# A streaming encoder layer on one core: loads moved on SyncE's queue, operand splits spread, rows scaled by VectorE

## The chip, the cores and the metric

One core of a Trainium2 chip. Its engines run side by side, each through its own instruction queue in order: TensorE (PE; weight loads PEld), VectorE (DVE), ScalarE (ACT), GpSimd (POOL) and SyncE (SP), which here issues the DMA transfers. The metric is the device time of one execution in microseconds.

## The reference, cut to what matters

One layer over 2048 tokens of width 1024, all in float32:

```python
h = x * (1.0 + sc1) + sh1
proj = einsum('bsd,de->bse', h, w_in)             # u, q, k, v
y_pool = pool_mixer(u, w_pool, pool_scale)        # trailing means, 4 windows
y_attn = chunked_attention(q, k, v, rel_bias)     # 64-token chunks, 9-chunk band, 8 heads
y = einsum('bse,ed->bsd', concatenate([y_pool, y_attn]), w_out)
x = layer_norm(ALPHA * x + (1.0 + g1) * y, ln1_g, ln1_b)
h = x * (1.0 + sc2) + sh2
f = square(relu(einsum('bsd,df->bsf', h, w_ff1)))  # width 4096
f = einsum('bsf,fd->bsd', f, w_ff2)
x = layer_norm(ALPHA * x + (1.0 + g2) * f, ln2_g, ln2_b)
```

The six vectors sh, sc, g come from the conditioning vector c.

## The kernel before

A float32 product is made of three matmuls in a reduced type: each operand is split into a high part (ScalarE casts it) and a low part (VectorE, or GpSimd in the first stage, subtracts the high part from the source). `split` writes both; one split of a 128x1024 tile is one cast and one subtraction (L59, L60).

Four stages follow each other. The order of instructions on each engine is the order in which the code issues them; a helper `after(n, f)` keeps a call back until `tick` has counted n further steps.

1. **Input projection and attention** (to about 680 us). The change leaves it as it is.
2. **Output projection and first layer norm** (about 680 to 857 us): 16 tiles t of 128 tokens. Of each, two halves n of 512 columns are 24 matmuls each (`wout_half`, L385), then `residual` adds x (tile `xt`, L872), `ln1_head` takes statistics (VectorE), four values (GpSimd, L782 to L784) and the normalised rows n (ScalarE, L785). `ln1_turn(u)` transposes a tile u, three tiles behind t at first, on TensorE and scales it into `h` on ScalarE (L831). `ln1_sums(u)` makes, for tiles 4 to 7 of a half of the tokens, four combinations with the rows of the partner tile (`hp`, loaded by `ln1_load` into a tile named w, L821; combinations L854 to L857) for the seven-product scheme of the next stage. The projection's left operands are streamed: `Stream` loads item j+2 into one of two `raw` buffers as soon as item j has been split (`dma_to` in `split_some`, L74); item t+2 is split at the start of tile t.
3. **First half of the MLP** (about 857 to 1502 us): 32 groups g of hidden columns, and for each group seven products s (a seven-product scheme over 2x2 blocks; `product`, L1041, 12 matmuls each). Product s multiplies a weight piece (split by `w_split`) with operand s (`hslot[s]`), a split tile. Products 0, 2, 4, 6 add into one PSUM bank and 1 (alone), 3, 5 into others, so between them `evacuate` copies a bank out (ScalarE, L1048) or adds it to a copy (VectorE, L1054). Groups 0 to 15 use the first 1024 tokens, groups 16 to 31 the other tokens, whose seven operands lie in DRAM and are loaded and split by `refill(i)` while group 15 runs: the load at product (15, i), the two splits one product later. Operand 4 of the first tokens is loaded after tile 15 (`op_load(4)`) and split in product (0,1), operand 6 in (0,4).
4. **Second half of the MLP and second layer norm** (about 1502 us to the end): 56 groups e of 48 matmuls (`issue`, L1322), 28 for each half of the tokens. In group e four splits are issued for group e+2 (`f2_split`), loads go four items ahead. Eight rows tiles `acc` (four named acc, four in g) hold ALPHA * x scaled by ln1_g (`ag`) plus ALPHA * ln1_b (`ab`): `load_acc` loads a tile from xS and GpSimd multiplies and adds (L1279, L1280). `take` adds finished banks to them (L1327). From e = 24 on `finish` makes the second layer norm of a tile (statistics L1287, L1299, L1303), stores it and loads the other tokens' rows into its place. A list `todo` of such generators is worked off in up to four steps per group.

Of the kernel before, what the change touches and what calls it, by code (L numbers as in the profile page):

```python
# [8 lines left out]
F32 = mybir.dt.float32  # L9
# [15 lines left out]
def trunk_layer(ctx: ExitStack, tc: tile.TileContext, xT, x, wada1, wada2, vecs, rows, win, wfirst, wpT, wout,  # L25
# [36 lines left out]
    class Stream:  # L62
        def __init__(self):
            self.items, self.raw, self.hl = [], {}, {}
            self.n_dma = self.n_split = 0

        def add(self, src, low, mul=None, dst=None):
# [14 lines left out]
        def split_some(self, i):  # L82
            while self.n_split <= min(i, len(self.items) - 1):
                j = self.n_split
                self.n_split += 1
                self.dma_to(j)
                r = self.raw.pop(j)
                _, low, mul, dst = self.items[j]
                if mul is not None:
                    mul(r)  # L90
                hl = dst() if dst else stream.tile([128, 2, 1024], F32R, name="hl", tag="hl", bufs=3)
                self.hl[j] = hl
                for c in range(0, 1024, 512):
                    split(hl[:, 0, c:c + 512], hl[:, 1, c:c + 512], r[:, c:c + 512], low)
                    yield
                self.dma_to(j + 2)

# [17 lines left out]
    late = {}  # L115
# [238 lines left out]
    def run(g):  # L354
        for _ in g:
            pass
# [418 lines left out]

    def norm(z, n):
        s6 = small.tile([128, 2, 6], F32, name="s6", bufs=3)
        for i in range(2):
            nc.vector.bn_stats(s6[:, i, :], z[:, i * 512:i * 512 + 512])
        mv = small.tile([128, 4], F32, name="mv", bufs=3)  # L780
        nc.vector.bn_aggr(mv[:, 0:2], s6)
        nc.gpsimd.tensor_scalar(mv[:, 1:2], mv[:, 1:2], EPS, 1.0, op0=ALU.add, op1=ALU.mult)  # L782
        nc.gpsimd.tensor_tensor(mv[:, 2:3], mv[:, 1:2], mhalf, op=ALU.pow)
        nc.gpsimd.tensor_scalar(mv[:, 3:4], mv[:, 0:1], mv[:, 2:3], -1.0, op0=ALU.mult, op1=ALU.mult)  # L784
        nc.scalar.activation(n, z, AF.Identity, bias=mv[:, 3:4], scale=mv[:, 2:3])  # L785

# [87 lines left out]
    def ln1_head(t):  # L874
        n_tiles[t] = ln.tile([128, 1024], F32, name="n", bufs=3)
        norm(xt.pop(t), n_tiles[t])
        if t + 2 < 16:
# [48 lines left out]

    def op_load(i):

        ops[i] = []
        for c in range(2):  # L930
            r = stream.tile([128, 1024], F32, name="raw", tag="raw", bufs=2).rearrange("p (r k c) -> p r k c", r=2, k=4)
            nc.sync.dma_start(r, h_piece(0, i, 2 * c, 2))
            ops[i].append(r)
# [17 lines left out]
    TURNS = {t: (t - 3,) if t < 11 else (2 * t - 14, 2 * t - 13) if t < 13 else (t - 1,) for t in range(3, 15)}  # L951
    waiting = []
    for t in range(3, 15):
        yc = st.get(yi[t]).rearrange("p a (k c) -> p a k c", k=8)
# [27 lines left out]
    ps = [dbank() for _ in range(2)]  # L982
    ln1_load(14)
    w_split(0, 0)
    for kh in range(2):
# [3 lines left out]
        if kh == 0:  # L989
# [3 lines left out]
            op_split(3)  # L993
            w_split(0, 1)
        tick(6)
    for n in range(2):
# [3 lines left out]
    w_load(1, late["w"])  # L1000
    op_load(4)
    ln1_sums(14, 1)
# [132 lines left out]

    def refill(i):

        hslot[i] = slot(i, "h2")
        if i % 2:
            r = ffp.tile([128, 4, 4, 128], F32, name="tw", tag="tw", bufs=1)  # L1140
            nc.sync.dma_start(r, h_piece(1, i, 0, 4))
            parts = [r[:, 0:2], r[:, 2:4]]
        else:
            parts = []
            for c in range(2):
                r = stream.tile([128, 1024], F32, name="raw", tag="raw", bufs=2).rearrange("p (r k c) -> p r k c", r=2, k=4)
                nc.sync.dma_start(r, h_piece(1, i, 2 * c, 2))
                parts.append(r)
        yield
        for c in range(2):  # L1150
            op_put(i, c, parts[c])

    back, refills = [], []

# [28 lines left out]
    for g in range(32):  # L1183
        for s in range(7):
            product(g, s)
            tick()
            if g == 0:
                if s == 1:
                    op_split(4)
                    ln1_load(15)  # L1190
                    op_load(6)
                elif s == 2:
# [32 lines left out]
            evacuate(g, s)  # L1225
            if (g, s) == (0, 0):
                w_split(0, 2)

# [16 lines left out]
            if back and next(back[0], "end") == "end":  # L1245
                back.pop(0)
            if (g == 15 and s) or (g, s) == (16, 0):
                if refills:
                    run(refills.pop())
            if g == 15:  # L1250
                refills.append(refill(s))
                next(refills[0])
            if g == 31 and s >= 3:
# [21 lines left out]
    def load_acc(b, t):  # L1275
        acc[t] = f2l.tile([128, 1024], F32, name=f"acc{t}") if t < 4 else gs[:, 2 * t - 8:2 * t - 6, :].rearrange(
            "p a c -> p (a c)")
        nc.sync.dma_start(acc[t], xS[b][t * 128:t * 128 + 128, :])
        nc.gpsimd.tensor_mul(acc[t], acc[t], late["ag"])  # L1279
        nc.gpsimd.tensor_add(acc[t], acc[t], late["ab"])  # L1280

# [47 lines left out]
    def finish(b, t):  # L1329
# [5 lines left out]
        outs.pop(t)()  # L1335
        yield

    todo = []
    for b in range(2):
        for i in range(7):  # L1340
            for kq in range(4):
# [18 lines left out]
                if e == 1:  # L1360
# [3 lines left out]
                    for t in range(8):  # L1364
                        load_acc(0, t)
                if e == 2:
                    late["l2g"] = row(f2l, rows[4:5], "r1")
                    late["l2b"] = row(f2l, rows[5:6], "r2")
                for _ in range(4):
                    if todo and next(todo[0], "end") == "end":  # L1370
                        todo.pop(0)
# [62 lines left out]
```

## Time and profile before

| | |
|---|---|
| median of three runs | 2141.13 us (2140.64 to 2142.0) |
| the profiled execution | 2148.31 us, span 2146.5 us |
| mean granted TensorE clock | 0.988 |
| TensorE busy | 2054.8 us (96%) |
| VectorE busy | 1324.2 us (62%) |
| ScalarE busy | 1002.8 us (47%) |
| GpSimd busy | 429.5 us (20%) |

The times of single instructions come from the profiled execution, and its span with what lies around it is 7.2 us over the median. TensorE's matmuls are pipelined, so a busy TensorE isn't by that at its best pace; the number of matmuls in stretches of equal length tells more. A wait is put down to what ended last before it. Idle time of the other engines costs nothing by itself.

### The profile page before, as it was taken

The numbers are of one execution on the slowest core, as the hardware profiler recorded it, in microseconds if no ns is written. First come the engines' busy times: TensorE is split into PE (matmuls) and PEld (weight loads), VectorE is DVE, ScalarE is ACT, GpSimd is POOL, SyncE is SP. The second block draws the span as 40 slices with busy tenths as digits, with TensorE's granted clock in tenths as the row PEclk, the third lists the DMA queues.
The fourth block names the chain that finished last, engine by engine and source line by source line (L and its number), as shares of the span: only waits on it lengthen the run. The fifth ranks groups of instructions, "written<-read, shape, count | busy, mean of one in ns | idle before, by whom it ended". The sixth has DMA issues, their size and how long they took to land. (4 is left out here: it accounts for less than half of the span.)

```text
span 2146.5 us, 27078 instructions
## 1 busy us (share of the span) xinstructions
PE 2054.8 (96%) x9672; PEld 1691.9 (79%) x9672; DVE 1324.2 (62%) x1926; ACT 1002.8 (47%) x1592; POOL 429.5 (20%) x474
## 2 busy tenths in 40 slices
PE   7999989999999999899999899999999999989998
PEld 6778867888877877678887788888778888878886
DVE  7555555556664454777767666666595449974448
ACT  4454555555553536545555555555444333343330
POOL 1535353553332000000000000000360004510002
PEclk9999999999999999999999999999999999999999
DMA  7444443444433557878878888887967556675542
GB/s 295 137 134 124 149 139 108 134 124 131 127 124 111 182 191 305 302 266 311 295 278 300 275 287 282 302 291 262 354 216 245 190 177 216 225 274 184 189 167 108
DMA packets 210361, 456.69 MB, mean 213 GB/s; under 512 B 18609, under 2 KB 36529, under 8 KB 209202
## 3 DMA queue, kind: packets, MB, share of 16 engines
q1 hardware_dynamic: 210226, 454.96, 62.5%
q8 instruction: 76, 1.25, 0.2%
q14 instruction: 59, 0.48, 0.1%
HBM read 294.45 MB, written 152.05 MB: 208 GB/s over the span
## 5 line engine op out<-in xcount | busy, mean ns | idle before, releaser
L1322 PE MATMUL f<-sb,sa 128*128 128x512 f32 x2688 | 624.7, 395 | 10.4 <-DVE sb L60 10.0
L1322 PEld LDWEIGHTS f<-sb,sa 128*128 128x128 f32 x2688 | 507.6, 189 | 127.3 <-DVE sb L60 12.4
L421 PE MATMUL d<-hT,hl 128*128 128x512 f32 x1392 | 373.0, 400 | 1.9 <-ACT vt L316 1.9
L1041 PE MATMUL f<-h,hl 128*128 128x512 f32 x1536 | 364.6, 393 | 6.2 <-ACT c L1048 6.2
L1041 PEld LDWEIGHTS f<-h,hl 128*128 128x128 f32 x1536 | 289.8, 189 | 72.3 <-ACT c L1048 7.0
L1041 PE MATMUL f<-sb,hl 128*128 128x512 f32 x1152 | 281.6, 398 | 10.3 <-ACT c L1048 6.2
L421 PEld LDWEIGHTS d<-hT,hl 128*128 128x128 f32 x1392 | 248.9, 189 | 42.3 <-ACT vt L316 2.3
L1041 PEld LDWEIGHTS f<-sb,hl 128*128 128x128 f32 x1152 | 219.4, 191 | 61.5 <-ACT c L1048 7.5
L635 DVE TENSOR_TENSOR PT<-T,PT 128x640 fp32r<-128x640 f32 (+4 forms) x128 | 94.9, 741 | 217.9 <-ACT PT L634 215.8
L612 ACT ACTIVATE s<-s,m 128x640 f32<-128x640 f32 (+4 forms) x128 | 98.0, 765 | 221.9 <-DVE m L610 170.8
L385 PE MATMUL d<-hT,hl 128*128 128x512 f32 x696 | 169.0, 400 | 4.1 <-DVE xt L872 4.1
L1063 ACT ACTIVATE g<-g 128x512 f32<-128x512 f32 x96 | 60.8, 633 | 211.6 <-DVE g L1054 211.6
L385 PEld LDWEIGHTS d<-hT,hl 128*128 128x128 f32 x696 | 131.5, 192 | 32.1 <-DVE xt L872 4.3
L618 POOL TENSOR_SCALAR s<-s,m 128x640 f32<-128x640 f32 (+4 forms) x128 | 96.5, 754 | 241.7 <-DVE m L617 199.2
L59 ACT CAST sb<-hl 128x1024 fp32r<-128x1024 f32 x67 | 70.4, 1050 | 152.2 <-PE f L1322 128.8
L60 DVE TENSOR_TENSOR sb<-hl,sb 128x1024 fp32r<-128x1024 f32 x67 | 95.1, 1420 | 73.8 <-ACT sb L59 73.5
L60 DVE TENSOR_TENSOR hl<-wsum,hl 128x1024 fp32r<-128x1024 f32 x64 | 78.4, 1225 | 95.2 <-ACT hl L59 95.1
L1363 POOL TENSOR_SCALAR ag<-ag 128x1024 f32<-128x1024 f32 x1 | 1.3, 1306 | 673.2 <-DMA acc<-xS 673.2
L60 DVE TENSOR_TENSOR sb<-raw,sb 128x1024 fp32r<-128x1024 f32 x55 | 84.6, 1544 | 54.7 <-ACT sb L59 54.5
L59 ACT CAST sb<-raw 128x1024 fp32r<-128x1024 f32 x55 | 57.4, 1051 | 114.1 <-PE f L1322 87.7
L1291 POOL TENSOR_SCALAR zv<-zv 128x1 f32<-128x1 f32 x16 | 18.4, 1150 | 449.8 <-DVE zv L1290 449.8
L60 DVE TENSOR_TENSOR hl<-w,hl 128x1024 fp32r<-128x1024 f32 x64 | 61.3, 958 | 70.0 <-ACT hl L59 70.0
(178 smaller groups left out, 2785.4 us busy)
## 6 DMA issues: line engine op xcount, KB each, us to landing
fS<-g SPq DMA_DIRECT2D x224, 256.0 KB, 3.6
hl<-fS SPq DMA_DIRECT2D x67, 512.0 KB, 4.6
hl<-tS SPq DMA_DIRECT2D x67, 512.0 KB, 4.5
w<-in_w_dram SPq DMA_DIRECT2D x48, 512.0 KB, 4.2
raw<-fS SPq DMA_DIRECT2D x45, 512.0 KB, 4.5
raw<-tS SPq DMA_DIRECT2D x45, 512.0 KB, 4.5
wS<-wsum SPq DMA_DIRECT2D x32, 512.0 KB, 4.9
raw<-in_w_dram SPq DMA_DIRECT2D x32, 512.0 KB, 5.3
```

Source lines behind the costliest of these rows:

```text
L59: nc.scalar.copy(hl_h, src)
L60: low.tensor_sub(hl_l, src, hl_h.bitcast(F32))
L385: nc.tensor.matmul(ps, yc[:, a, k, :], hT(b, k, cols), start=(k == 0 and i == 0), stop=(k == 7 and i == 2))
L421: nc.tensor.matmul(ps, w[name][:, a, k, :], hT(b, k, slice(tb * 512, tb * 512 + 512)), start=(n == 0), stop=(n == 23))
L612: nc.scalar.activation(s[:, 0:w], s[:, 0:w], AF.Exp, bias=m[:, 0:1], scale=-1.0, accum_out=m[:, 1:2])
L618: nc.gpsimd.tensor_scalar(s[:, 0:nk * 128], s[:, 0:nk * 128], m[:, 1:2], 1.0, op0=ALU.mult, op1=ALU.mult)
L635: nc.vector.tensor_sub(ol, src, oh.bitcast(F32))
L1041: nc.tensor.matmul(ps, w[:, p, c:c + 128], h[:, q, k, :], start=first and k == 0 and (p, q) == (0, 0), stop=k == 3 and p == 1, skip_group_ ...
L1063: nc.scalar.activation(o, o, AF.Relu)
L1291: nc.gpsimd.tensor_scalar(mv[:, 1:2], mv[:, 1:2], EPS, 1.0, op0=ALU.add, op1=ALU.mult)
L1322: nc.tensor.matmul(bank, f, w, start=start, stop=stop, skip_group_check=True)
L1363: nc.gpsimd.tensor_scalar(r, r, ALPHA, 1.0, op0=ALU.mult, op1=ALU.mult)
```

## The change

Four things.

- **Stream loads.** In stage 2 `Stream.defer` becomes `after(6, f)`: the load of item j+2 is issued at the end of the first half of tile t rather than directly behind the split at its start.
- **Operand 4 and tile 15.** Operand 4 of the first tokens is loaded into one tile of the ring `n` at the start of tile 15 and one of the ring `xt` in its middle, and split directly behind `ln1_head(15)`. `op_load(6)` takes the old place of `op_load(4)`. `norm` now returns the normalising activation instead of issuing it, and for tile 15 it is issued behind the copy of product (0,0).
- **Other tokens' operands.** `refill` is gone. With q = 7 (g - 15) + s counting products from (15,0), loads stand at q = -2, -1, 2, 4, 6, 7, 9 and the splits at q = 1, 3, 5, 6, 8, 10, 11. Operand i is used at q = 7 + i.
- **Rows.** The multiplication and the addition on `acc` move from GpSimd to VectorE, as two steps of a generator `scale_acc` in `todo`. Three steps are worked off per group from e = 4 to 51, four otherwise, and a generator that ends no longer uses up a step.

```diff
+            self.defer = lambda f: f()
@@ split_some
-                self.dma_to(j + 2)
+                self.defer(lambda: self.dma_to(j + 2))
@@ norm
-        nc.scalar.activation(n, z, AF.Identity, bias=mv[:, 3:4], scale=mv[:, 2:3])
+        return lambda n: nc.scalar.activation(n, z, AF.Identity, bias=mv[:, 3:4], scale=mv[:, 2:3])
@@ ln1_head
-        norm(xt.pop(t), n_tiles[t])
+        apply = norm(xt.pop(t))
+        if t == 15:
+            late["n"] = lambda: apply(n_tiles[t])
+        else:
+            apply(n_tiles[t])
@@ op_load
-        for c in range(2):
-            r = stream.tile([128, 1024], F32, name="raw", tag="raw", bufs=2).rearrange("p (r k c) -> p r k c", r=2, k=4)
-            nc.sync.dma_start(r, h_piece(0, i, 2 * c, 2))
+        for t in tiles or [stream.tile([128, 1024], F32, name="raw", tag="raw", bufs=2) for _ in range(2)]:
+            r = t.rearrange("p (r k c) -> p r k c", r=2, k=4)
+            nc.sync.dma_start(r, h_piece(0, i, 2 * len(ops.setdefault(i, [])), 2))
...
+    st.defer = lambda f: after(6, f)
     for t in range(3, 15):
...
     ln1_load(14)
+    op_load(4, [ln.tile([128, 1024], F32, name="n", bufs=3)])
     w_split(0, 0)
...
             op_split(3)
             w_split(0, 1)
+            op_load(4, [ln.tile([128, 1024], F32, name="xt", bufs=2)])
...
     w_load(1, late["w"])
-    op_load(4)
+    op_load(6)
+    op_split(4)
     ln1_sums(14, 1)
@@ refill becomes refill_load (the loads alone)
+    LOADS = {-2: 0, -1: 1, 2: 2, 4: 3, 6: 4, 7: 5, 9: 6}
+    SPLITS = {1: 0, 3: 1, 5: 2, 6: 3, 8: 4, 10: 5, 11: 6}
@@ loop over g and s
                 if s == 1:
-                    op_split(4)
                     ln1_load(15)
-                    op_load(6)
...
             if (g, s) == (0, 0):
+                late["n"]()
                 w_split(0, 2)
...
-            if (g == 15 and s) or (g, s) == (16, 0):
-                if refills:
-                    run(refills.pop())
-            if g == 15:
-                refills.append(refill(s))
-                next(refills[0])
+            q = 7 * (g - 15) + s
+            if q in SPLITS:
+                op_split(SPLITS[q])
+            if q in LOADS:
+                refill_load(LOADS[q])
@@ load_acc
-        nc.gpsimd.tensor_mul(acc[t], acc[t], late["ag"])
-        nc.gpsimd.tensor_add(acc[t], acc[t], late["ab"])
+
+    def scale_acc(t):
+        nc.vector.tensor_mul(acc[t], acc[t], late["ag"])
+        yield
+        nc.vector.tensor_add(acc[t], acc[t], late["ab"])
+        yield
@@ finish
         outs.pop(t)()
         yield
+        if b == 0:
+            yield from scale_acc(t)
@@ loop over e
                     for t in range(8):
                         load_acc(0, t)
+                        todo.append(scale_acc(t))
...
-                for _ in range(4):
-                    if todo and next(todo[0], "end") == "end":
+                for _ in range(4 if e < 4 or e >= 52 else 3):
+                    while todo and next(todo[0], "end") == "end":
                         todo.pop(0)
```

What moves, in the order of the queues. SyncE, stage 2, around tile 9; raw<-yS is the stream load, w<-hP the partner's rows, xS and hP are stores. Before:

```order
L761 DMA xt_7174<-in_x_dram 128x1024
L74 DMA raw_7228<-yS1_66 128x1024
L821 DMA w_7230<-hP00_81 128x1024
L825 DMA xS0_125<-n_7014 128x1024
L862 DMA hP02_83<-w_7126 128x1024
L863 DMA hP01_82<-w_7164 128x1024
L761 DMA xt_7279<-in_x_dram 128x1024
```

Now:

```order
L762 DMA xt_7172<-in_x_dram 128x1024
L75 DMA raw_7174<-yS1_66 128x1024
L822 DMA w_7228<-hP00_81 128x1024
L826 DMA xS0_125<-n_7014 128x1024
L863 DMA hP02_83<-w_7124 128x1024
L864 DMA hP01_82<-w_7162 128x1024
L762 DMA xt_7277<-in_x_dram 128x1024
L75 DMA raw_7279<-yS1_66 128x1024
```

The raw load that a tile's own split releases stood ahead of that tile's w load (raw_7228 ahead of w_7230); now it stands five rows later, behind the next xt load (raw_7279 behind w_7228), and the raw load ahead of the w load is the one of the tile before.

ScalarE at the passage from stage 2 to stage 3: `sb<-raw` and `sb<-n`, `sb<-xt` are casts of operands, `n<-xt` the normalisation of tile 15, `c<-f` the copy of product (0,0), `h<-T` the scaling behind the transposes of tile 15. Before:

```order
L59 CAST sb<-raw 128x2x4x128 x2
L59 CAST hl<-wsum 128x1024
L785 ACTIVATE n<-xt,mv 128x1024
L1048 COPY c<-f 128x512
L59 CAST hl<-wsum 128x1024
L59 CAST sb<-raw 128x2x4x128 x2
L831 ACTIVATE h<-T,b_6606,a_6605 128x128 x8
```

Now:

```order
L59 CAST sb<-raw 128x2x4x128 x2
L59 CAST hl<-wsum 128x1024
L59 CAST sb<-n 128x2x4x128
L59 CAST sb<-xt 128x2x4x128
L1056 COPY c<-f 128x512
L786 ACTIVATE n<-xt,mv 128x1024
L59 CAST hl<-wsum 128x1024
L832 ACTIVATE h<-T,b_6606,a_6605 128x128 x8
```

Operand 4's casts moved from behind the copy to ahead of it, the normalisation from ahead to behind.

VectorE in stage 4, where the first half's tiles are finished (sa, sb are splits, ag and ab the scaling of a reloaded row, n<-g and n<-n the layer norm). Before:

```order
L1287 BN_STATS z_14687<-acc_13060 128x6 x2
L1290 BN_AGGR zv<-z_14687 128x2
L1299 SCALAR_TENSOR_TENSOR n<-acc_13060,zv,r_13149 128x1024
L1303 SCALAR_TENSOR_TENSOR n<-n,zv,r_13151 128x1024
L60 TENSOR_TENSOR sa<-hl,sa 128x1024
L60 TENSOR_TENSOR sb<-hl,sb 128x1024
L60 TENSOR_TENSOR sa<-hl,sa 128x1024
L60 TENSOR_TENSOR sb<-raw,sb 128x1024
```

Now:

```order
L1296 BN_STATS z_14981<-acc_13062 128x6 x2
L1299 BN_AGGR zv<-z_14981 128x2
L1308 SCALAR_TENSOR_TENSOR n<-acc_13062,zv,r_13137 128x1024
L1312 SCALAR_TENSOR_TENSOR n<-n,zv,r_13139 128x1024
L60 TENSOR_TENSOR sa<-hl,sa 128x1024
L60 TENSOR_TENSOR sb<-hl,sb 128x1024
L60 TENSOR_TENSOR sa<-raw,sa 128x1024
L60 TENSOR_TENSOR sb<-raw,sb 128x1024
L1286 TENSOR_TENSOR acc_14991<-acc_14991,ag 128x1024
L1288 TENSOR_TENSOR acc_14991<-acc_14991,ab 128x1024
L1296 BN_STATS z_15061<-g 128x6 x2
L1299 BN_AGGR zv<-z_15061 128x2
```

Between the splits of two groups stood one tile's layer norm; now three steps stand there, of which the scaling of a reloaded row makes two.

## Rows read from the trace of the kernel before

**Rows 1.** Waits of TensorE: total us, times, longest us.

```profile
PE f L1041 <- ACT c L1048: 12.4, 5, 3.6
PE f L1322 <- DVE sb L60: 10.0, 6, 6.0
```

**Rows 2.** Stretches: length, busy us (count) by engine, clock, DMA share, GB/s.

```profile
1050.00:1100.00 50.00, 50.00 (x220) 40.98 (x219) 37.62 (x51) 23.98 (x37) 0.00 (x0) 1.00 0.77 273
...
1150.00:1200.00 50.00, 44.38 (x181) 35.55 (x180) 35.40 (x40) 33.52 (x44) 0.00 (x0) 0.93 0.88 310
1200.00:1250.00 50.00, 47.84 (x202) 38.67 (x202) 31.94 (x41) 25.02 (x38) 0.00 (x0) 0.97 0.82 285
...
1550.00:1600.00 50.00, 47.78 (x206) 38.27 (x205) 46.63 (x23) 20.21 (x20) 39.34 (x13) 1.00 0.65 221
...
1600.00:1650.00 50.00, 50.00 (x220) 41.04 (x219) 33.55 (x33) 24.63 (x24) 0.00 (x0) 1.00 0.73 252
...
1850.00:1900.00 50.00, 44.04 (x181) 35.59 (x180) 45.37 (x34) 16.18 (x16) 23.27 (x12) 0.93 0.70 237
...
1950.00:2000.00 50.00, 50.00 (x216) 40.51 (x215) 21.55 (x20) 18.13 (x18) 0.00 (x0) 1.00 0.54 179
```

**Rows 3.** Timeline of TensorE, stages 2 to 3: start, length us; idle before, releaser.

```profile
794.27 7.38 PE L385 MATMUL d<-hT,hl 128*128 128x512 f32 x24 [4.11 <-DVE xt L872]
...
811.59 1.45 PE L828 MATMUL T<-ident,n 128*128 128x128 f32 x8 [3.54 <-ACT w L831]
...
866.70 4.62 PE L1041 MATMUL f<-h,hl 128*128 128x512 f32 x12 [3.61 <-ACT c L1048]
...
877.41 4.41 PE L1041 MATMUL f<-sb,hl 128*128 128x512 f32 x12 [2.46 <-ACT c L1048]
```

**Rows 4.** Timeline of TensorE, group 15, products 5 and 6.

```profile
1175.90 2.93 PE L1041 MATMUL f<-h,hl 128*128 128x512 f32 x12
1181.87 5.49 PE L1041 MATMUL f<-sb,hl 128*128 128x512 f32 x12 [3.04 <-DVE g L1054]
```

**Rows 5.** Timeline of SyncE's queue in stage 2.

```profile
776.16 0.32 SPq L74 DMA_DIRECT2D raw<-yS  x1
776.58 0.38 SPq L821 DMA_DIRECT2D w<-hP  x1
...
793.65 0.32 SPq L74 DMA_DIRECT2D raw<-yS  x1
...
850.97 0.32 SPq L825 DMA_DIRECT2D xS<-n  x1
```

**Rows 6.** Timeline of VectorE in stage 2: the first combination behind the w load.

```profile
783.75 0.69 DVE L854 TENSOR_TENSOR w<-w 128x512 f32<-128x512 f32 x1 [6.42 <-issue]
```

**Rows 7.** Tile acc: time from a load's issue to its landing.

```profile
DMA to landing us min/median/max: 3.3/6.3/11.1
```

**Rows 8.** Timeline of ScalarE between stages 2 and 3.

```profile
864.94 1.24 ACT L785 ACTIVATE n<-xt,mv 128x1024 f32<-128x1024 f32 x1 [7.03 <-POOL mv L784]
866.08 0.56 ACT L1048 COPY c<-f 128x512 f32<-128x512 f32 x1
```

**Rows 9.** Timeline of ScalarE in group 15: the casts of operand 3.

```profile
1182.96 1.99 ACT L59 CAST sb<-tw 128x1024 fp32r<-128x1024 f32 x2 [3.20 <-DMA tw<-hP]
```

**Rows 10.** Timeline of VectorE in stage 4, groups 25 to 27.

```profile
1784.50 3.43 DVE L60 TENSOR_TENSOR sa<-raw,sa 128x1024 fp32r<-128x1024 f32 x1
...
1791.22 1.27 DVE L1287 BATCH_NORM_STATS2 z<-acc 128x6 f32<-128x512 f32 x2
...
1797.12 1.22 DVE L60 TENSOR_TENSOR sb<-hl,sb 128x1024 fp32r<-128x1024 f32 x1
...
1804.96 1.27 DVE L1287 BATCH_NORM_STATS2 z<-acc 128x6 f32<-128x512 f32 x2
```

**Rows 11.** Timeline of GpSimd in stage 4: the first scaling, and one of a reloaded row.

```profile
1540.66 2.41 POOL L1279 TENSOR_TENSOR acc<-acc,ag 128x1024 f32<-128x1024 f32 x1
...
1784.07 2.78 POOL L1279 TENSOR_TENSOR acc<-acc,ag 128x1024 f32<-128x1024 f32 x1 [3.08 <-DMA acc<-xS]
```

More of the change, by code (lines that the diff above doesn't have):

```diff
@@ L774, in trunk_layer, with norm @@
     nc.vector.tensor_add(b2, b2, mods[:, 0, :])
-    def norm(z, n):
+    def norm(z):
         s6 = small.tile([128, 2, 6], F32, name="s6", bufs=3)
@@ L925, in trunk_layer, with op_load @@
     ops = {}
-    def op_load(i):
-        ops[i] = []
-        for c in range(2):
-            r = stream.tile([128, 1024], F32, name="raw", tag="raw", bufs=2).rearrange("p (r k c) -> p r k c", r=2, k=4)
-            nc.sync.dma_start(r, h_piece(0, i, 2 * c, 2))
+    def op_load(i, tiles=()):
+        for t in tiles or [stream.tile([128, 1024], F32, name="raw", tag="raw", bufs=2) for _ in range(2)]:
+            r = t.rearrange("p (r k c) -> p r k c", r=2, k=4)
+            nc.sync.dma_start(r, h_piece(0, i, 2 * len(ops.setdefault(i, [])), 2))
             ops[i].append(r)
@@ L1134, in right_halves, with refill_load @@
             nc.sync.dma_start(tS[i][p], s)
-    def refill(i):
-        hslot[i] = slot(i, "h2")
+    LOADS = {-2: 0, -1: 1, 2: 2, 4: 3, 6: 4, 7: 5, 9: 6}
+    SPLITS = {1: 0, 3: 1, 5: 2, 6: 3, 8: 4, 10: 5, 11: 6}
+    def refill_load(i):
         if i % 2:
@@ L1141, in refill @@
             nc.sync.dma_start(r, h_piece(1, i, 0, 4))
-            parts = [r[:, 0:2], r[:, 2:4]]
+            ops[i] = [r[:, 0:2], r[:, 2:4]]
         else:
-            parts = []
+            ops[i] = []
             for c in range(2):
@@ L1147, in refill @@
                 nc.sync.dma_start(r, h_piece(1, i, 2 * c, 2))
[L1148 to L1153, printed above, removed]
+                ops[i].append(r)
+    back = []
     f2_items = [(b, i, kq, c, kind) for b in range(2) for i in range(7) for kq in range(4) for c in range(2)
```

## The prediction

> **What bounds the kernel now.** TensorE: it is busy 96% of the span and issues at a fixed pace, so I looked for the stretches in which it doesn't. First the list of what it waited for [rows 1]: the long entries are ScalarE's copies out of PSUM between the seven products, and VectorE's splits in the last stage. Then the stretches of equal length [rows 2]: undisturbed ones hold 220 matmuls in 50 us, so one costs 50 / 220 = 0.2273 us. The two from 1150 to 1250 us hold 57 too few, 1550 to 1600 holds 14 too few, 1850 to 1900 holds 39 too few. Such a stretch has two losses: the wait, and TensorE's clock, whose mean is 0.93 in two of them against 1.00. Twelve matmuls take 2.93 us at the full clock, and 4.62 us right after a wait of 3.61 us [rows 3, 4]: behind a wait of over 2 us I add 1.7 us. From 1950 us on a third thing shows: 216 matmuls in 50 us, at a clock of 1.00 and with no wait [rows 2]. This slow pace follows the stretch at 1850.
>
> **Part 1, stream loads half a tile later.** In the projection stage SyncE's queue holds, tile by tile, the load into raw and then the load of the partner rows into w. The raw load can't issue before a split has emptied its buffer, and the w load stands behind it: it issued at 776.58 us, right after raw at 776.16; the next raw load issued at 793.65, 17.49 us later [rows 5]. VectorE waited 6.42 us for those rows, until 783.75 us [rows 6]; only behind its four combinations stand the tile's statistics, GpSimd's three small steps, ScalarE's normalisation and the next split. So the circle split, raw load, w load, combination, split takes 17.5 us, while a tile's 48 matmuls and 8 transposes take 48 x 0.2273 plus about 1, some 12 us. TensorE's waits of 4.11 and 3.54 us [rows 3] are this lag. In the new order raw stands behind xt, so the w load stands behind a split of the tile before. The raw load is still one and a half tiles (18 us) ahead of its use, and landings of 512 KB took 3.3 to 11.1 us [rows 7]. Without the 6.42 us the circle is 17.49 - 6.42 = 11.1 us, under 12. Gain: 4.11 + 3.54 + 2 x 1.7 = **11.05 us**. Late next is the same circle, with 1 us to spare; if the w load is held by the store that frees its tile instead, the gain goes to 0.
>
> **Part 2, operand 4 early, normalisation of tile 15 late.** Product (0,2) adds into the bank that ScalarE must first copy out. ScalarE stood at the normalisation of tile 15 (n<-xt), which started at 864.94 us after 7.03 us of waiting for GpSimd; the copy started at 866.08 [rows 8], and product (0,2) at 866.70 after 3.61 us [rows 3]. Product (0,0) had ended one product earlier than that wait began, at 863.1 - 2.9 = 860.2. Now two casts of operand 4 stand ahead of the copy and the normalisation behind it. They need a load into n and one into xt; the second is queued on SyncE behind the store of tile 14, which issued at 850.97 [rows 5]. If it lands within some 7 us the copy is on time; if it takes 11.1, copy, normalisation and the cast of wsum stand behind it and most of the old wait is back. What is late next: the transposes of tile 15 need the normalisation at about 866.2, 0.5 us after product (0,2) ends. The 2.46 us in front of product (0,4) [rows 3] stay, since its copy stands behind those transposes in both orders. On VectorE the two splits move ahead of ln1_sums(14) and of the split of wsum, 2.4 us that pass before product (0,4) needs them. The loads of operand 6 move up and meet a free raw buffer. Gain: 3.61 + 1.7 - 0.5 = **4.8 us** (0 to 6).
>
> **Part 3, operands of the second half over eleven products.** Before, all seven are loaded and split while products (15,0) to (16,0) run. A split is two casts (1.99 us) and two subtractions (1.22 us each); ScalarE stood 3.20 us waiting for one load [rows 9, 10]. The copies and additions that free the banks stood behind, and TensorE waited, 3.04 us among others [rows 4]. The loss is 57 x 0.2273 = 13.0 us. The work stays: 14 casts, 14 us, on top of ScalarE's usual 23.98 in 50 us [rows 2], 14.4 in the 30 us of eleven products. Going through the new order product by product with these durations I get four waits: 0.4 us in front of (15,6), whose bank waits for an addition behind operand 1; 1.5 in front of (16,2), whose copy stands behind the casts of operand 3; 1.2 at (16,5), since operand 5 is cast only when (16,3) has been copied out and takes 0.2 + 0.5 + 2.0 + 1.2 = 3.9 us against one product of 2.7; and 1.9 at (16,6) for operand 6, which follows it through both engines. Sum 5.0 us, each too short for the clock as I take it. Gain **8.0 us**. Ends: 13.0 if these overlap better than worked out, 3.1 if a load is late by 3.20 us again and one wait brings the clock down (5.0 + 3.2 + 1.7 left).
>
> **Part 4, rows scaled by VectorE.** GpSimd made 32 operations on 128x1024 rows. While one runs, a split's subtraction takes 3.43 us, alone 1.22 [rows 10]. One finished tile took VectorE 1804.96 - 1791.22 = 13.74 us [rows 10], more than a group's 48 x 0.2273 = 10.9, so its lead shrank until TensorE stood for 6.0 us [rows 1]. Now: 13.74 - 2 x (3.43 - 1.22) + 2 x 1.22 = 11.8 us per finished tile, 4.9 of it four splits; a tile takes five steps at three per group, so a group costs 4.9 + 0.6 x 6.9 = 9.0 us of 10.9. The added wait: each multiplication stands on VectorE until its row is loaded, and the splits, hence TensorE, stand behind it. For five of the second half's eight tiles the order puts load and multiplication into the same group. GpSimd waited 3.08 us for such a row [rows 11], landings were 3.3 to 11.1 [rows 7]: 15 to 55 us in all, against 1.9 us per group over 13 groups (25 us) and a lead of two groups (22 us). Mostly covered. In the first half VectorE waits in group 1 until the first row is there, 1540.66 us at the latest [rows 11], again with a lead of two groups. So both losses go: 14 x 0.2273 = **3.2 us** and 39 x 0.2273 = **8.9 us**. The slow pace (50 / 216 - 50 / 220 = 4.2 ns a matmul, for the 1030 from there to the end) began with the wait, and I take it to go too: **4.3 us**, or 0.
>
> **Sum.** 11.05 + 4.8 + 8.0 + 3.2 + 8.9 + 4.3 = 40.2 us. The profiled execution took 2148.31 us, 7.2 above the median of 2141.13; it would come to 2108.1, the median to **2100.9 us**.
>
> **Rivals.** (a) The pace stays at 216 whatever the waits: 2105.2. For it: no row shows its cause. Against: it begins with the wait. (b) Part 3 makes new waits with late loads: 2100.9 + 4.9 = 2105.8. For it: ScalarE is at 14 + 14.4 of 30 us there. (c) The w load of part 1 waits for its own tile's store: 2112. Against: that store is issued a tile earlier. (d) Reloads at the head of VectorE's queue use up its lead, and much of the 8.9 and the 4.3 us stays: about 2110. (e) VectorE becomes the bound of the last stage: if the 32 operations, 32 x 1.22 = 39 us, all lengthen the path in place of the 12.1 us of waits, the time is 2141.1 - 23.9 + 26.9 = 2144. Against: the subtraction of 3.43 us beside GpSimd. A rule for it, in the Trainium skill, "Perfetto Trace Analysis", section Optimizing Scalar/DVE Operations: a saturated VectorE may be relieved by moving work to GpSimd, the reverse of this part, though, it adds, the two share a read port and it might not help. By that first half the time would be this rival's; the row of 3.43 us sides with the second.
>
> (f) Slower: the mechanism of (d) at full size. If each of the eight reloads holds VectorE for its landing w, 8w less the 47 us of cover falls on TensorE; from w = 10.4 us on that eats parts 1 to 3, the 3.2 and the 8.9 us (36 us), from 10.9 on the kernel is 0.2% slower, and at 11.1 it takes 2147 us. Only the longest landing is that long [rows 7]. That the change doesn't do what it says I leave out: the order shows each move.
>
> **Chances.** Forecast 0.50; (a) 0.17, (b) 0.11, (c) 0.08, (d) 0.07, (e) 0.02, two or more of (a) to (d) together (2110 to 2125) 0.03, (f) 0.02. The range from 2092 (part 3 gains all of its 13.0, part 2 its 6, the rest a little more) to 2116 ((c) with part of (b)) leaves out under 2 in 10. A measurement of this kernel can tell about 0.2% (4.3 us) from no change: faster 0.95, within 0.03, slower 0.02.
>
> **What would show it.** Right: no wait of 4 us for xt; the copy ahead of the normalisation at product (0,2); 210 or more matmuls in each 50 us around the refill, its waits at (16,2), (16,5), (16,6); no subtraction of 3.43 us and 220 matmuls in every 50 us of the last stage, to its end. Wrong: the w load still 6 us late, casts of operand 4 waiting for xt, VectorE standing over 8 us for acc or g, or 216 matmuls with no wait before them.

## The result, and the profile after

| | before | after |
|---|---|---|
| median | 2141.57 us (4 runs, 2140.64 to 2144.93) | 2113.74 us (4 runs, 2111.92 to 2119.41) |
| profiled execution | 2148.31 us | 2112.46 us, span 2110.6 |
| mean granted TensorE clock | 0.988 | 0.994 |
| GpSimd busy | 429.5 us | 333.3 us |

The ratio is 0.9871 [0.9857, 0.9884]: 27.8 us in the medians, forecast 40.2. The two profiled executions lie 35.9 us apart. So two things have to be explained: 8 us that the profiles show and the medians don't, and some 4 that neither shows. Measured a second time beside other runs, the medians lay 31.4 us apart (2145.41 and 2113.98, ratio 0.9856 [0.9840, 0.9873]), most of the difference in the kernel before; so a difference of 3 us between medians isn't to be read as an effect of the change.

TensorE's waits of after, which answer to [rows 1] (total us, times, longest us):

```profile
PE f L1049 <- ACT c L1056: 9.3, 3, 5.8
PE f L1331 <- DVE sb L60: 1.8, 2, 1.0
PE f L1049 <- ACT sb L59: 1.6, 1, 1.6
```

The waits for splits in the last stage fell from 10.0 to 1.8 us. The copies out of PSUM still cost 9.3, and the longest wait for one is now 5.8 us, where it was 3.6. The stretches of 50 us of after (busy us and count by engine, clock, DMA share, GB/s), as in [rows 2]:

```profile
1050.00:1100.00 50.00, 50.00 (x220) 40.98 (x219) 34.41 (x46) 26.02 (x40) 0.00 (x0) 1.00 0.81 284
1150.00:1200.00 50.00, 45.49 (x193) 35.57 (x192) 37.66 (x41) 35.92 (x49) 0.00 (x0) 1.00 0.93 329
1200.00:1250.00 50.00, 50.00 (x220) 40.93 (x218) 31.50 (x40) 25.20 (x38) 0.00 (x0) 1.00 0.85 294
1550.00:1600.00 50.00, 50.00 (x220) 41.04 (x219) 38.01 (x35) 24.94 (x24) 0.00 (x0) 1.00 0.82 282
1850.00:1900.00 50.00, 50.00 (x220) 41.04 (x219) 38.75 (x40) 17.88 (x17) 2.58 (x4) 1.00 0.72 242
1950.00:2000.00 50.00, 50.00 (x220) 41.02 (x219) 24.47 (x24) 18.08 (x18) 0.00 (x0) 1.00 0.57 189
```

Read the count behind the first busy time, the number of matmuls: only one of these stretches is short of 220 now, the one of the refill (193), and its clock is 1.00.

TensorE issues the same 9672 matmuls in the same order in all but two of the kernels here (the two in which tile 15 is moved back), so the start of the n-th one can be subtracted between two traces. What a stretch gained (minus) or lost against the first trace of before, in us, stretches by that trace's time:

| kernel | 740 to 862 | 862 to 933 | 1150 to 1250 | 1550 to 1600 | 1880 to 1900 | 1900 to end |
|---|---|---|---|---|---|---|
| after | -11.3 | +1.5 | -6.7 | -3.1 | -9.0 | -4.5 |
| after, again | -11.3 | -0.9 | -6.6 | -3.1 | -9.0 | -4.5 |
| before, again | -1.4 | +0.6 | -1.8 | -0.9 | -0.6 | -4.5 |
| part 1 alone | -11.4 | +1.1 | -2.4 | +0.3 | -0.7 | -4.5 |
| part 2 alone | -0.9 | +1.5 | -2.4 | -0.4 | -1.0 | -4.5 |
| part 3 alone | +0.3 | +2.4 | -5.9 | +0.6 | -0.2 | -4.5 |
| part 4 alone | -1.7 | +1.5 | -2.2 | -3.1 | -9.0 | -4.5 |
| after without part 2 | -11.3 | +2.8 | -5.4 | -3.1 | -9.0 | -4.5 |

The first trace of before is one execution, and the last column shows what that means: whatever is changed, or nothing, 4.5 us are gone. The other columns scatter too: where a kernel has nothing of a part, its column differs from the first trace by up to 1.7 us in the first, 2.8 in the second and 2.4 in the third.

### The profile page after: what moved, and what is told of

Read it like the earlier page. It is cut to its first block, busy times and chain, and to the rows that moved or that the text cites. A ratio compares the mean times of both kernels' runs of the same rounds, so it can differ in the third digit from the quotient of the medians.

```text
span 2110.6 us, 27080 instructions
## 1 busy us (share of the span) xinstructions
PE 2037.9 (97%) x9672; PEld 1681.5 (80%) x9672; DVE 1303.0 (62%) x1958; ACT 1001.5 (47%) x1592; POOL 333.3 (16%) x442
## 4 chain that ended last, share of the span: by engine, by line
PE 81%; DVE 7%; ACT 4%; DMA 3%; issue 3%; POOL 2%; SPq 0%; DVEq 0%; POOLq 0%; ACTq 0%
PE f L1331 26%; PE f L1049 26%; PE d L422 10%; PE d L386 6%; PE pv L648 3%; PE T L627 2%; PE S L604 2%; DVE s L611 1%; ACT PT L635 1%; PE d L169 1%; DMA raw<-in_wada_dram 1%; DVE PT L636 1%; DVE sb L60 1%; PE S L169 1%; PE S L386 1%
## 5 line engine op out<-in xcount | busy, mean ns | idle before, releaser
L1331 PE MATMUL f<-sb,sa 128*128 128x512 f32 x2688 | 616.3, 391 | 2.1 <-DVE sb L60 1.8
L1049 PE MATMUL f<-sb,hl 128*128 128x512 f32 x1152 | 279.7, 396 | 11.6 <-ACT c L1056 8.1
L60 DVE TENSOR_TENSOR sb<-hl,sb 128x1024 fp32r<-128x1024 f32 x67 | 81.9, 1222 | 69.0 <-ACT sb L59 68.8
L604 PE MATMUL S<-k,q 128*128 128x320 f32 (+1 forms) x448 | 92.2, 322 | 12.8 <-DVE m L611 12.7
```

The lines of the kernel that those rows point to most:

```text
L60: low.tensor_sub(hl_l, src, hl_h.bitcast(F32))
L604: nc.tensor.matmul(S[:, 512 * p:512 * p + wp], q[:, i * 128:i * 128 + 128], k[:, a, k0 + p * wp:k0 + p * wp + wp], start=(a == 0), stop=(a ...
L1049: nc.tensor.matmul(ps, w[:, p, c:c + 128], h[:, q, k, :], start=first and k == 0 and (p, q) == (0, 0), stop=k == 3 and p == 1, skip_group_ ...
L1331: nc.tensor.matmul(bank, f, w, start=start, stop=stop, skip_group_check=True)
```

## The four parts, each alone

Each kernel is before with one part of the diff. Part 1 is the stream loads: three lines of the diff (`self.defer`, its call in `split_some`, `st.defer`) and nothing else.

> The kernel before with the stream loads half a tile later and nothing else. Theory A (each part works alone, and the gains of the parts add up; in the trace of the changed kernel TensorE is 11.5 us earlier at the end of the projection stage than at its start): 2141.6 - 11.5 = 2130 us, no wait of TensorE for xt over 1 us, and the waits of the next stage as before (3.6 us in front of product (0,2)). Rival B (the lag of the projection stage is given back at the passage to the next stage, because operand 4 and the stores behind tile 15 then become late): 2136 us or more, with a wait in front of products (0,2) or (0,4) that is longer than before by 5 us.

Measured: 2132.23 us, ratio 0.9946 [0.9930, 0.9963], 11.6 us by the ratio. Theory A holds: the gain is there in every kernel with this part, to 0.1 us. The waits in front of products (0,2) and (0,4) are those of before, 3.63 and 2.45 us, so rival B is out; only the twelve matmuls behind the first take longer, 5.40 us where [rows 3] has 4.62:

```profile
856.40 5.40 PE L1043 MATMUL f<-h,hl 128*128 128x512 f32 x12 [3.63 <-ACT c L1050]
...
867.88 4.59 PE L1043 MATMUL f<-sb,hl 128*128 128x512 f32 x12 [2.45 <-ACT c L1050]
```

The stretches of this kernel at the wait of 6.0 us in the last stage, which it keeps, and behind it:

```profile
1850.00:1900.00 50.00, 44.04 (x184) 35.66 (x183) 43.04 (x36) 21.47 (x21) 15.67 (x8) 0.93 0.76 260
1950.00:2000.00 50.00, 50.00 (x220) 41.03 (x219) 26.00 (x24) 18.23 (x18) 0.00 (x0) 1.00 0.63 205
```

The wait and the low clock are there (184 matmuls, 0.93), and the pace behind them is 220, not 216. So the wait alone doesn't make the slow pace.

Part 2 is operand 4 and tile 15: the edits of `norm`, `ln1_head`, `op_load` and their calls, with `op_split(4)` ahead of `ln1_sums(14, 1)`.

> The kernel before with operand 4 loaded beside tile 15 and split behind it, and the normalisation of tile 15 behind the copy of product (0,0), nothing else. Theory A (the two splits of operand 4 stand on VectorE ahead of the sums of tile 14, so the store that frees the tile h is issued later, the eight activations h<-T of tile 15 wait for it, and the copy for product (0,4) stands behind them): no gain, 2141.6 + 1.5 = 2143 us; no wait of 3.6 us in front of product (0,2), but one of over 4 us in front of (0,4), and ScalarE's h<-T waiting for the store out of h. Rival B (the prediction's part 2; the wait at (0,4) comes only of TensorE being earlier through part 1): 2141.6 - 4.8 = 2136.8 us, a wait of about 2.5 us in front of (0,4).

Measured: 2141.68 us, ratio 0.9989 [0.9979, 0.9999]. Theory A has the mechanism, but not the size: it expected a loss of 1.5 us, and by the ratio the part gains 2.4 us, 0.2 to 4.5 by the interval. TensorE, then ScalarE (start us, duration, operation, what it waited for):

```profile
876.21 5.08 PE L1047 MATMUL f<-sb,hl 128*128 128x512 f32 x12 [5.88 <-ACT c L1054]
```

```profile
871.09 2.90 ACT L831 ACTIVATE h<-T,b,a 128x128 f32<-128x128 f32 x8 [3.74 <-DMA hP<-h]
```

Rival B is out: without part 1 the wait in front of (0,4) is 5.88 us too.

Part 3 is `refill_load`, `LOADS` and `SPLITS` in place of `refill`.

> The kernel before with the other tokens' operands loaded and split over eleven products, nothing else. Theory A (the part's gain is its own): 2141.6 - 6.7 = 2134.9 us (the prediction's 8.0 would be 2133.6); waits of about 1.2 us at product (16,2), 0.7 at (16,5), 2.3 at (16,6), clock 1.00 from 1150 to 1250 us. Rival B (the gain hangs on part 2 or on the earlier clock): under 3 us, 2139 us or more.

Measured: 2140.05 us, ratio 0.9981 [0.9967, 0.9994], 4.1 us by the ratio, between the two theories, and 1.3 to 7.1 by the interval, which leaves both in. The table says more: the trace gains 5.9 us against the first trace of before, but each kernel that keeps the old refill gains 1.8 to 2.4 there as well, so that the part is worth 3.5 to 4.1.

Part 4 is the two operations on VectorE, as steps of `todo`, together with the new count of steps per group; no run has the one without the other.

> The kernel before with the rows scaled by VectorE in place of GpSimd, nothing else. Theory A (the two waits of the last stage go, and the slow pace of 216 matmuls in 50 us belonged to the one profiled execution and not to the usual ones): 2141.6 - 3.1 - 9.0 = 2129.5 us, 220 matmuls in every stretch of 50 us of the last stage. Rival B (the slow pace is in every execution of the kernel before and goes as well): 2141.6 - 16.4 = 2125.2 us. Rival C (the pace stays at 216 whatever the waits): 2129.5 us with 216 matmuls in each of the last stretches.

Measured: 2132.05 us, ratio 0.9944 [0.9927, 0.9960], 12.0 us by the ratio: theory A's 12.1, and 220 matmuls or more in each of its stretches from 1550 to 2100 us. A subtraction of the form sb<-hl,sb takes 1222 ns there, as in after.

## The kernel before, a second time

No edit.

> The kernel before, unchanged, for a second profiled execution. Theory A (the first profiled execution was itself some 7 us over the median by things that other executions don't have: the slow pace of 216 matmuls per 50 us from 1888 us on, 4.5 us, and one more period at the low clock around product (16,3), 2.3 us): span about 2140, 220 matmuls in each stretch of 50 us after 1900, still the wait of 6 us near 1880. Rival B (the slow pace belongs to the kernel before): 216 again behind the wait, span about 2146.

Measured: 2140.81 us, span 2139.0. Its stretches:

```profile
1200.00:1250.00 50.00, 50.00 (x219) 40.92 (x218) 31.06 (x40) 27.32 (x42) 0.00 (x0) 1.00 0.85 294
1850.00:1900.00 50.00, 44.04 (x183) 35.62 (x182) 45.33 (x34) 17.47 (x17) 21.89 (x10) 0.93 0.73 245
1950.00:2000.00 50.00, 50.00 (x220) 41.04 (x219) 26.27 (x26) 18.08 (x18) 0.00 (x0) 1.00 0.51 169
```

Theory A holds. Beside [rows 2]: the second stretch of the refill is full (219, clock 1.00, where the first trace had the lower clock and fewer), the wait at 1880 has stayed, the slow pace has not come. The slow pace (4.5 us) and the extra period at the low clock (1.8 to 2.4) make 6.3 to 6.9 of the 7.2 us by which the first trace was over its median. How often executions that weren't profiled have either isn't known.

## The passage between the stages

In after, TensorE (first fence) waits 5.84 us in front of product (0,4) for ScalarE's copy c. ScalarE (second) stands in front of the eight activations h<-T until a store out of h has landed; SyncE (third) issued that store at 853.40, behind the combinations on VectorE (fourth), and these behind the two splits of operand 4:

```profile
852.56 1.09 PE L829 MATMUL T<-ident,n 128*128 128x128 f32 x8 [0.80 <-ACT n L786]
853.41 3.02 PE L1049 MATMUL f<-sb,hl 128*128 128x512 f32 x12
862.26 4.47 PE L1049 MATMUL f<-sb,hl 128*128 128x512 f32 x12 [5.84 <-ACT c L1056]
```

```profile
851.27 1.24 ACT L786 ACTIVATE n<-xt,mv 128x1024 f32<-128x1024 f32 x1 [4.26 <-POOL mv L785]
...
857.14 2.90 ACT L832 ACTIVATE h<-T,b,a 128x128 f32<-128x128 f32 x8 [3.69 <-DMA hP<-h]
...
861.63 1.06 ACT L1056 COPY c<-f 128x512 f32<-128x512 f32 x2
```

```profile
853.40 0.43 SPq L864 DMA_DIRECT2D hP<-h  x1
```

```profile
848.12 1.20 DVE L60 TENSOR_TENSOR sb<-n,sb 128x1024 fp32r<-128x1024 f32 x1
849.24 1.22 DVE L60 TENSOR_TENSOR sb<-xt,sb 128x1024 fp32r<-128x1024 f32 x1
850.37 0.69 DVE L855 TENSOR_TENSOR hp<-h,hp 128x512 f32<-128x512 f32 x1
```

There is one tile named h for tiles 14 and 15 (`bufs=1` in `h_tile`), so tile 15's rows can't be written to it before tile 14's have left. The first test puts the sums ahead of the splits:

```diff
-    op_split(4)
     ln1_sums(14, 1)
+    op_split(4)
```

> The changed kernel with ln1_sums(14) issued ahead of the two splits of operand 4 rather than behind them. Theory A (the wait of 5.84 us in front of product (0,4) comes from the store out of h, which the sums release and which stood 2.4 us later behind the two splits): the store goes out 2.4 us earlier, the wait falls to about 3.4 us, the period at the low clock may fall from 6.83 to 3.41 us: 2113.7 - 2.4 to 4.1 = 2110 to 2111 us. Rival B (the landing of the store is held by the DMA queues, whenever it is issued, or ScalarE waits for something else): wait and time unchanged, 2113 to 2114 us.

Measured: 2114.02 us, 0.9875 [0.9834, 0.9915]; one of the four runs took 2130.66 us, hence the wide interval. SyncE's store and ScalarE's activations:

```profile
852.02 0.42 SPq L864 DMA_DIRECT2D hP<-h  x1
```

```profile
857.09 2.90 ACT L832 ACTIVATE h<-T,b,a 128x128 f32<-128x128 f32 x8 [2.08 <-DMA hP<-h]
```

Half of A, half of B: against the matmuls the store went out 2.2 us earlier, but its bytes came in 5.1 us after the issue instead of 3.7, so the wait in front of (0,4) fell by 1.6 us only, to 4.22. The trace is 2.9 us better than that of after from 862 to 933, but after's own second trace is 2.4 us better there with no edit, and the time shows nothing. The second test keeps this edit and also takes h<-T out of the copy's way:

```diff
-                elif s == 2:
-                    ln1_turn(15)
...
             evacuate(g, s)
+            if (g, s) == (0, 2):
+                ln1_turn(15)
```

> As sums_first, and the eight activations h<-T of tile 15 stand on ScalarE behind the copy of product (0,2) instead of ahead of it. Theory A: nothing stands ahead of that copy that waits for a store; the wait of 5.84 us and the low clock behind it go, 5.84 + 3.4 = 9.2 us, to 2104.5 us (2108 if the copy of product (0,3), now behind h<-T, makes a wait of 1.5 us and a period at the low clock stays). Rival B (another buffer or the additions of product (0,4) are late as well): 2110 us or more.

Measured: 2112.98 us, 0.9852 [0.9831, 0.9872]. The wait of 5.84 us fell to 1.26, as A has it, but 2.92 us, with the low clock behind them, came up in front of (0,6): the addition of product (0,4) was late instead, as B has it. The third test keeps the first edit too and moves all of tile 15 back:

```diff
-                elif s == 2:
-                    ln1_turn(15)
-                elif s == 3:
-                    ln1_sums(15, 1)
...
                 elif s == 5:
+                    ln1_sums(15, 1)
...
             evacuate(g, s)
+            if (g, s) == (0, 3):
+                ln1_turn(15)
             if (g, s) == (0, 0):
+                w_split(0, 2)
                 late["n"]()
-                w_split(0, 2)
```

> The changed kernel with tile 15, which nothing needs before the second half, moved back: ln1_sums(14) ahead of the splits of operand 4, the split of the weight sum for product (0,4) ahead of the normalisation of tile 15, the transposes and h<-T of tile 15 behind the copy of product (0,3), its sums behind product (0,5). Theory A (all waits at the passage are ScalarE and VectorE standing at something of tile 15 ahead of a copy or an addition): no wait over 1 us in front of products (0,2) to (0,6) and no low clock there, 7 us less than the changed kernel: 2106.5 us. Rival B (the copies are late for another reason, or the stores of tile 15 now collide with the next group): 2111 us or more.

Measured: 2113.19 us, 0.9853 [0.9838, 0.9867], B. TensorE, and VectorE:

```profile
860.40 3.02 PE L1049 MATMUL f<-sb,hl 128*128 128x512 f32 x12 [1.69 <-ACT c L1056]
...
868.86 4.48 PE L1049 MATMUL f<-sb,hl 128*128 128x512 f32 x12 [2.70 <-DVE g L1062]
...
906.61 4.60 PE L1049 MATMUL f<-sb,hl 128*128 128x512 f32 x12 [2.09 <-ACT c L1056]
```

```profile
864.61 2.36 DVE L60 TENSOR_TENSOR sb<-raw,sb 128x1024 fp32r<-128x1024 f32 x2 [2.70 <-ACT sb L59]
866.89 1.22 DVE L60 TENSOR_TENSOR hl<-w,hl 128x1024 fp32r<-128x1024 f32 x1
868.03 0.68 DVE L1062 TENSOR_TENSOR g<-f,c 128x512 f32<-128x512 f32 x1
```

Now the addition that frees the bank of (0,4) stands behind the splits of operand 6, and these behind h<-T on ScalarE. From the start of product (0,0) to the end of (0,6), after has for its engines (busy us and count):

```profile
843.39:873.30 29.91, 22.29 (x93) 17.43 (x92) 21.58 (x29) 15.87 (x26) 2.69 (x3) 0.89 0.80 290
```

Seven products and the transposes of tile 15 take TensorE about 20 us without a wait (an estimate from 84 x 0.2273 and 0.85 us). VectorE's 21.6 us are more than that, ScalarE's 15.9 are not. In the two orders that took most from the wait in front of (0,4), one of 2.7 to 2.9 us came up in front of (0,6); that no order avoids it is not shown. A fourth test, on top of the third, the gate one group later (`if g == 2` for `if g == 1`), was for the wait of 2.09 us at product (2,4):

> As tile15_later, and the gate's weighted sum (nine loads into raw, a step on VectorE per product) begins one group later. Theory A (the wait of 2.2 us at product (2,4) comes of loads into raw that are late because tile 15's stores are still under way): that wait and the low clock behind it go, 2 us less than tile15_later. Rival B (the loads are late wherever they stand, one product after another): the same wait one group later, the same time.

Measured: 2113.36 us, 0.9853 [0.9838, 0.9868]: the wait at (2,4) is gone, 1.44 us without the low clock stand at (3,4) instead, and the time is the same: B, with a shorter wait than it expected. At last, after without part 2 (the edits of part 2 above, reversed), beside after itself:

> The changed kernel with part 2 undone: operand 4 loaded behind tile 15 and split in product (0,1), operand 6 loaded there, the normalisation of tile 15 ahead of the copy of product (0,0). Theory A (part 2 gains nothing; from 862 to 933 us the kernel with part 1 alone loses 1.1 us, the changed kernel 1.5): equal to the changed kernel within 1 us, 2113 us, with a wait of over 5 us in front of product (0,2) or (0,4) as with part 1 alone. Rival B (the forecast's 4.8 us are there, hidden in the scatter): 2118.5 us.

> The changed kernel again, unchanged, beside the next two. Its profiled execution shows how much of its trace repeats: the wait in front of product (0,4) (5.84 us), those of the refill (1.2, 0.7, 1.6 and 0.8 us), no stretch under 220 matmuls in the last stage. 2113.7 us if the earlier runs are typical.

Measured: 2114.90 us without part 2, 0.9861 [0.9845, 0.9876], and 2113.98 us with it, 0.9856 [0.9840, 0.9873]: equal within 1 us, as theory A has it. The wait of over 5 us that A names isn't there, here or in part 1 alone:

```profile
853.03 4.60 PE L1042 MATMUL f<-h,hl 128*128 128x512 f32 x12 [3.60 <-ACT c L1049]
...
863.72 4.57 PE L1042 MATMUL f<-sb,hl 128*128 128x512 f32 x12 [2.45 <-ACT c L1049]
```

Two waits, 6.05 us, against 5.84 and the 0.80 in front of the transposes in after. What part 2 gains comes of the clock: without it the granted clock is 0.50 from 853.4 to 856.8 us and from 863.7 to 867.1, nearly all of it on matmuls; in after it is 0.50 from 858.6 to 865.4, and 3.7 us of that lie inside the wait. The forecast's 4.8 us aren't there; about 1 us is, by these medians, too little for these runs to tell from none.

## The refill one product earlier

The waits of after there, on TensorE and then ScalarE:

```profile
1166.57 3.02 PE L1049 MATMUL f<-sb,hl 128*128 128x512 f32 x12 [0.24 <-DVE g L1062]
...
1176.25 3.04 PE L1049 MATMUL f<-h,hl 128*128 128x512 f32 x12 [1.19 <-ACT c L1056]
...
1186.07 2.79 PE L1049 MATMUL f<-h,hl 128*128 128x512 f32 x11 [0.74 <-DVE h L60]
1190.44 0.50 PE L1049 MATMUL f<-sb,hl 128*128 128x512 f32 x1 [1.58 <-ACT sb L59]
1191.70 2.80 PE L1049 MATMUL f<-sb,hl 128*128 128x512 f32 x11 [0.76 <-DVE sb L60]
```

```profile
1186.79 1.05 ACT L59 CAST sb<-raw 128x1024 fp32r<-128x1024 f32 x1 [1.27 <-DMA raw<-hP]
1189.35 1.04 ACT L59 CAST sb<-raw 128x1024 fp32r<-128x1024 f32 x1 [1.51 <-DMA raw<-hP]
```

Operand 6 is cast as its loads land. On top of turn_behind_copy:

```diff
-    LOADS = {-2: 0, -1: 1, 2: 2, 4: 3, 6: 4, 7: 5, 9: 6}
+    LOADS = {-2: 0, -1: 1, 2: 2, 4: 3, 5: 4, 6: 5, 8: 6}
```

> As turn_behind_copy, and operands 4, 5 and 6 of the other tokens are loaded one product earlier (q = 5, 6, 8 instead of 6, 7, 9). Theory A (the waits of 1.6 and 0.8 us in front of product (16,6) are ScalarE's waits for the loads of operand 6, 1.3 and 1.5 us): 2.3 us less, and the 0.7 us at (16,5) may go: 2102 us. Rival B (operand 6 is limited by the casts on ScalarE, not by the loads, or SyncE's queue stands at the loads and holds up the weight loads behind): no gain, 2104 to 2106 us.

Measured: 2113.76 us, 0.9859 [0.9841, 0.9877], B: no gain on the 2112.98 us of turn_behind_copy. On TensorE, VectorE and SyncE, with what SyncE waited for (total us, times, longest us):

```profile
1184.00 5.49 PE L1049 MATMUL f<-sb,hl 128*128 128x512 f32 x12 [3.64 <-ACT c L1056]
```

```profile
1180.94 0.69 DVE L1062 TENSOR_TENSOR g<-f,c 128x512 f32<-128x512 f32 x1 [3.84 <-DMA fS<-g]
```

```profile
1167.52 1.49 SPq L1157 DMA_DIRECT2D raw<-hP  x2
1174.05 0.36 SPq L1151 DMA_DIRECT2D tw<-hP  x1
1174.46 1.88 SPq L1090 DMA_DIRECT2D fS<-g  x3
```

```profile
SPq L1151 <- DVE sb L60: 3.5, 1, 3.5
```

SyncE stood at the load into tw until 1174.05, since VectorE was still splitting operand 3 out of the one tile tw; the stores fS<-g stood behind, VectorE waited 3.84 us for one of them to free a g tile, and ScalarE and TensorE behind it. The waits at operand 6 shrank and a longer one stands ahead of them.

## Point by point

- **Part 1: right**, 11.3 for 11.05 us, in each of the traces that have it, against the first trace of before; against the traces that keep the old loads it is 9.6 to 11.6. No wait for xt is left; the 48 matmuls of a tile's two halves now take 11.25 us without a gap.
- **Part 2: wrong**, 1 to 2.4 for 4.8 us. The step that failed is "The 2.46 us in front of product (0,4) [rows 3] stay, since its copy stands behind those transposes in both orders". The copy stands behind them, yes, but the activations behind the transposes write h, and h is freed by a store that the sums of tile 14 release. I had moved two splits ahead of these sums and priced them by product (0,4)'s own operands alone. The wait of 2.46 became 5.84 us.
- **Part 3: its waits right, its gain too large**, 3.5 to 4.9 us by the traces for 8.0. The waits in after (0.24, 1.19, 0.74, 1.58 + 0.76 us) make 4.5 against the 5.0 worked out, at (15,6), (16,2), (16,5) and (16,6) as forecast, with the clock at 1.00. The step that failed is the loss before: "57 x 0.2273 = 13.0 us" was one execution's; others lose 1.8 to 2.4 us less there. And the stretch of the refill in after is 27 matmuls short, 6.1 us, 1.6 more than its waits; the forecast took the waits for the whole loss, and its sign, 210 or more matmuls in each stretch, was missed with 193.
- **Part 4: right**, 3.1 and 9.0 us against the first trace for 3.2 and 8.9. A subtraction takes 1.22 us now, 1.42 in the mean before (a group of VectorE over the last stage: its count, then busy us and mean ns; first before, then after):

```profile
L60 DVE TENSOR_TENSOR sb<-hl,sb 128x1024 fp32r<-128x1024 f32 x66 | 93.9, 1423 | 73.8 <-ACT sb L59 73.5
```

```profile
L60 DVE TENSOR_TENSOR sb<-hl,sb 128x1024 fp32r<-128x1024 f32 x61 | 74.6, 1222 | 68.8 <-ACT sb L59 68.8
```

  VectorE did wait for rows in after, 31.2 us in all (total us, times, longest us; then the longest of the first half's rows and of the reloaded ones):

```profile
DVE acc L1286 <- DMA acc<-xS: 17.4, 3, 8.9
DVE g L1286 <- DMA g<-xS: 13.8, 3, 6.9
```

```profile
1520.97 1.23 DVE L1286 TENSOR_TENSOR acc<-acc,ag 128x1024 f32<-128x1024 f32 x1 [8.87 <-DMA acc<-xS]
...
1861.44 1.23 DVE L1286 TENSOR_TENSOR g<-g,ag 128x1024 f32<-128x1024 f32 x1 [6.87 <-DMA g<-xS]
```

  The 8.87 us belong to the first row of the first half. The reloaded rows make the other 22.3, at five of eight tiles as forecast, within its 15 to 55. "VectorE standing over 8 us" was named as a sign of being wrong; it happened once, but TensorE has no wait at all from 1503 to 2100 us, so the sign was too strict and the cover against rivals (d) and (f) held. Rival (e) is out. The Trainium skill, "Perfetto Trace Analysis", section Optimizing Scalar/DVE Operations, says in the second half of the rule cited for it that VectorE and GpSimd share a read port, so that moving work between them might not help. The trace agrees: with GpSimd's work gone VectorE's subtractions of this form fell from 1423 to 1222 ns. That the port is the reason no run here shows.
- **The slow pace, 4.3 us: wrong.** "Began with the wait, and I take it to go too": thirteen other profiled executions don't have it, four of them with the wait of 6 us in place. The changed kernel was never seen with it, so rival (a) didn't come true either; but the time comes out 4.3 us longer just the same, since what the usual execution doesn't lose can't be gained.
- **The sum: the failing step** is "it would come to 2108.1, the median to 2100.9 us". It takes the whole 40.2 us off the median, though the excess of that execution over the median was made of two of the terms, the pace and part of the refill's loss. Of the 12.4 us between forecast and medians, 4.3 are the pace, 3 to 4.5 the refill, 2.5 to 4 part 2; the second measurement (31.4 us) leaves 8.8 to explain, so this division is no finer than some 3 us. The four parts measured alone add up to 11.6 + 2.4 + 4.1 + 12.0 = 30.1 us, the whole change by its two ratios gains 27.6 and 30.8: within the noise the parts add, and it was their sizes that were off. The 35.9 us between the two profiled executions flatter the forecast: beside the pace and the extra loss at the refill they hold 2.7 us that fell before 740 us, where after's second trace gained none.
- **The range.** 2113.74 us lies in it, near its upper end of 2116, and in part by luck: that end was made of rival (c) and part of (b), and neither happened. No rival named the wait for the store out of h, nor losses that only the profiled execution had.

## What to carry to other kernels

Before a loss in a trace is subtracted from a median, ask whether it is in a second trace of the same kernel; an execution that is 0.3% over its median may hold losses that a change to the kernel can't give back. Where work is moved ahead of other work on an engine, follow what the overtaken work releases, stores that free a buffer among it, to whatever stands at the head of the next queue. Where an engine is full at a passage, expect that a better order may only move the wait to a later product, as two of the orders tried here did; whether less work there, or a second tile h, would take it away no run here tests.

## What the runs showed of the hardware

The pace of 216 matmuls per 50 us at a granted clock of 1.00 came in one profiled execution of fourteen, and what sets it stays open. Four of the other thirteen have the same wait of 6 us. Unchanged, the kernel before spread from 2138.41 to 2150.65 us in 23 runs. And a wait's length doesn't fix the clock behind it: 2.09 us brought it down (the row at 906.61 above, 4.60 us for twelve matmuls), 2.38 us in the kernel with part 2 alone did not (3.02 us for twelve):

```profile
1182.59 3.02 PE L1047 MATMUL f<-sb,hl 128*128 128x512 f32 x12 [2.38 <-DVE g L1060]
```
